# A 512-column bfloat16 product ahead of each PSUM bank of the RWKV features, scores and inverses

## The chip, the cores and the metric

The kernel runs on one core of one Trainium2 chip, in one launch. The metric is the device time of that core in microseconds (us), the median of the runs shown; lower is better. The engines are called as in the profile: PE (TensorE, its matmuls), PEld (its weight loads), DVE (VectorE), ACT (ScalarE), POOL (GpSimd) and SP (SyncE, which issues transfers).

## The reference, cut to what matters

Two layers of a block that mixes 512 latent tokens and 256 context tokens of width 1024 by three mixers side by side (RWKV, S5 and window attention), and then sends them through 32 experts of which each token takes two. The part that the change touches is the RWKV mixer: 4 heads of width 64, in both directions of time.

```python
def step(s, inp):
    r_t, w_t, k_t, v_t, kk_t, b_t = inp
    s_kk = jnp.einsum('bhvk,bhk->bhv', s, kk_t)
    s = s * w_t[:, :, None, :] - s_kk[..., None] * b_t[:, :, None, :] + v_t[..., None] * k_t[:, :, None, :]
    return s, (jnp.einsum('bhvk,bhk->bhv', s, r_t) if emit else None)
```

The kernel doesn't scan token by token: it works in chunks of 64 tokens, for which it needs decayed features, triangular score matrices and the inverse of one of them.

## The kernel before, in words

A layer runs in this order: the input side (projections `proj` and S5), then one stage that holds RWKV, attention, the modulation products of later stages (`mod_unit`, which streams `w_mod` in slices of 128 columns) and the output mix, then the experts. In that stage everything lies in one program whose order on each engine a planner makes from the dependences; the calls only give the order in which the work is written down.

RWKV itself (`rwkv`, from line 327) goes over six tiles of 128 tokens, written down as tiles 0, 1, 2, 5, 3, 4:

- `front(i)`, line 367: the features of a tile. It takes six PSUM banks in turn: the two low-rank products against `wa` (lines 382 and 388, 512 columns each), two banks of transposes (line 59), the running sum of the decay (line 416) and its chunk totals (line 422, 2 columns). ACT, DVE and POOL work between them.
- `back(i)`, line 465: the scores of a tile. Five banks for each direction: two of transposes (line 59, copied out by ACT at lines 483 and 495), two of scores (line 503, masked by DVE at line 506) and one for the score times the values (line 515).
- `inverse(b)`, line 524: the inverses of the 32x32 triangles of three tiles in each direction, on DVE and POOL (lines 551 and 552).
- `solve(i, d)`, line 564: four banks, in which the inverses are put together to 64x64 (lines 585 and 592) and applied (lines 604 and 606).
- `step(n, d)`, `output` and `finish`, from line 616: the recurrence over 12 chunks in each direction, and what is written from it.

Every bank comes from `bank()`, line 46. It gives a tile of 128x512 float32 of the stream that is set: `FS` (`b_f`, 2 buffers) for `front`, `finish` and direction 0 of `solve` and `step`, `GS` (`b_g`, 2 buffers) for `back` and direction 1, `b_a` (4 buffers) for attention, modulation and the mix. A bank can be written again when the readers of its tile before have released it. `oneb` is a 128x128 bfloat16 tile of ones in SBUF.

`fill` (line 2167) writes down attention, modulation and mix work between the tiles of RWKV, so PE has other work in the same stage.

Of the kernel before, what the change touches and what calls it, by code (L numbers as in the profile page):

```python
# [10 lines left out]
F32 = mybir.dt.float32  # L11
# [19 lines left out]
class K:  # L31


    def __init__(self, tc, a):
        self.tc, self.nc, self.a = tc, tc.nc, a
        self.dr = {}
        self.win = {}
        self.free = []
        self.stream = ('m', 8)

    def dram(self, name, shape, dt=F32):
# [3 lines left out]

    def bank(self):

        return self.ps.tile([128, 512], F32, name='b_' + self.stream[0], tag='b_' + self.stream[0], bufs=self.stream[1])

    def pool(self, name, st, **kw):  # L50

# [3 lines left out]
def tr(k, out, x):  # L55

    n = x.shape[0]
    r = x.base_partition()
    k.nc.tensor.transpose(out, x, k.idf[r:r + n, r:r + n])  # L59
# [265 lines left out]
def rwkv(k, l, st, cvd, Y, ys, streams, fill):  # L325
# [40 lines left out]

    def front(i):

        out = emit_ctx or i >= 2
        k.stream = FS  # L370
        Cv = Fp.tile([128, 8, 128], F32, name='cvt', bufs=3)
# [85 lines left out]
        for d in range(2):  # L457
# [3 lines left out]
                q.dma_start(rec[z, :, r:r + 64, c:c + 256], src)  # L461
            nc.sync.dma_start(atd[z, :, 0], at[:, d, :])
        F[i] = at, rh, bt, kh

    def back(i):

        out = emit_ctx or i >= 2
        k.stream = GS
        at, rh, bt, kh = F.pop(i)
        n = 2 if out else 1  # L470
        j = len(done) % 2
        done.append(i)
        vv = vz[j]
        nc.scalar.dma_start(vv[0:64], rec[slot[i, 0], :, 0:64, 256:512].rearrange("c t x -> t c x"))
        for d in range(2):
            z = slot[i, d]

            ar = Fp.tile([128, 2, 2, 2, 64], F32, name='ar', bufs=2)
            p = k.bank()
            for s, src in ((0, at), (1, rh))[0:n]:  # L480
                for q in range(2):
                    tr(k, p[:, 256 * s + q * 128:256 * s + q * 128 + 128], src[:, d, q * 128:q * 128 + 128])
                A.copy(ar[:, s].rearrange("p c q t -> p q c t"), p[:, 256 * s:256 * s + 256].rearrange("p (q c t) -> p q c t", q=2, c=2))
            if out:
                nc.scalar.dma_start(rec[z, :, :, 640:768].rearrange("c p x -> p c x"), ar[:, 1].rearrange("p c q t -> p c (q t)"))

            bk = bz[(2 * j + d) % 2]
            p = k.bank()
            for s, src in ((0, bt), (1, kh)):
                for q in range(2):  # L490
                    tr(k, p[:, 256 * s + q * 128:256 * s + q * 128 + 128], src[:, d, q * 128:q * 128 + 128])
                pv = p[:, 256 * s:256 * s + 256].rearrange("p (q c t) -> p q c t", q=2, c=2)
                for hp in range(2):
                    r_ = slice(64 * hp, 64 * hp + 64)
                    A.copy(bk[r_, hp, :, :, 1 - s, :], pv[r_])  # L495

            sc = Fp.tile([128, 2, 2, 2, 2, 64], F32, name='sc', bufs=2)
            for hp in range(2):
                p = k.bank()
                pv = p.rearrange("p (c q s t) -> p c q s t", c=2, q=2, s=2)  # L500
                for q in range(2):
                    for cp in range(2):
                        nc.tensor.matmul(pv[:, cp, q, 0:n, :], bk[:, hp, q, cp].rearrange("p s t -> p (s t)"),  # L503
                                         ar[:, 0:n, cp, q, :], start=True, stop=True)
                for s in range(n):
                    V.tensor_tensor(sc[:, s, :, hp], pv[:, :, :, s, :], k.msk[d][:, None, s:s + 1, :].to_broadcast([128, 2, 2, 64]), op=ALU.mult)
            nc.sync.dma_start(sca[z].rearrange("a p t -> p a t"), sc[:, 0].rearrange("p c h q t -> p (c h q) t"))
            if out:
                nc.sync.dma_start(rec[z, :, :, 768:1024].rearrange("c p x -> p c x"), sc[:, 1].rearrange("p c h q t -> p c (h q t)"))

            p = k.bank()
            for h in range(4):
                q, hp = divmod(h, 2)
                for cp in range(2):
                    nc.tensor.matmul(p[64 * cp:64 * cp + 64, 64 * h:64 * h + 64], sc[:, 0, cp, hp, q, :], vv[:, cp, 64 * h:64 * h + 64], start=True, stop=True)
            r1 = Fp.tile([128, 256], F32, name='r1', bufs=2)
            A.copy(r1, p[:, 0:256])
            nc.scalar.dma_start(atd[z, :, 1], r1)

    def dblk(ap, s0, q):  # L520

        return bass.AP(tensor=ap.tensor, offset=ap.offset + s0 * 4096 + 2080 * q, ap=[[4096, 24], [64, 32], [1, 32]])
# [40 lines left out]

    def solve(i, d):

        k.stream = (FS, GS)[d]
        z = slot[i, d]
        s0 = z * 8
        u, v = 64 + 32 * d, 32 - 32 * d
        ab = Q.tile([128, 8, 32], F32, name='ab', bufs=SB)  # L570
        nc.sync.dma_start(ab[u:u + 32], sca[z, :, u:u + 32, v:v + 32].rearrange("a p t -> p a t"))
        at = Q.tile([128, 2, 256], F32, name='atl', bufs=SB)
        nc.scalar.dma_start(at, atd[z])
        x = Q.tile([128, 4, 64], F32, name='x', bufs=SB)
        for cp in range(2):
            nc.sync.dma_start(x[64 * cp:64 * cp + 64], inv_o[s0 + 4 * cp:s0 + 4 * cp + 4].rearrange("h i t -> i h t"))
        t = Q.tile([128, 8, 32], F32, name='xt', bufs=SB)
        nc.scalar.dma_start(t[u:u + 32], inv_t[s0:s0 + 8].rearrange("h i t -> i h t"))

        p = k.bank()  # L580
        w = Q.tile([128, 4, 32], F32, name='xw', bufs=2)
        for cp in range(2):
            v = 64 * cp + 32 - 32 * d
            for h in range(4):
                nc.tensor.matmul(p[v:v + 32, 32 * h:32 * h + 32], ab[u:u + 32, 4 * cp + h, :],
                                 t[u:u + 32, 4 * cp + h, :], start=True, stop=True, tile_position=(u, v))
            A.copy(w[v:v + 32], p[v:v + 32, 0:128].rearrange("p (h t) -> p h t", h=4))
        p = k.bank()
        for cp in range(2):
            u, v = 64 * cp + 32 * d, 64 * cp + 32 - 32 * d  # L590
            for h in range(4):
                nc.tensor.matmul(p[u:u + 32, 32 * h:32 * h + 32], w[v:v + 32, h, :], x[v:v + 32, h, 32 - 32 * d:64 - 32 * d],
                                 start=True, stop=True, tile_position=(v, u))
            V.tensor_scalar(x[u:u + 32, :, 32 - 32 * d:64 - 32 * d], p[u:u + 32, 0:128].rearrange("p (h t) -> p h t", h=4), -1.0, None, op0=ALU.mult)
        own = [slice(0, 64), slice(64, 128)]
        heads = [(hq, 2 * (hq % 2) + hq // 2) for hq in range(4)]

        xa = Q.tile([128, 2, 128], F32, name='xa', bufs=2)
        W = Q.tile([128, 2, 256], F32, name='W', bufs=1)
        for cp in range(2):  # L600
            p = k.bank()
            for hq, h in heads:
                hp, q = divmod(hq, 2)
                nc.tensor.matmul(p[64 * hp:64 * hp + 64, 64 * q:64 * q + 64], at[own[cp], 0, 64 * h:64 * h + 64], x[own[cp], hq, :], start=True, stop=True)
            for hq, h in heads:
                nc.tensor.matmul(p[64:128, 256 + 64 * h:320 + 64 * h], x[own[cp], hq, :], at[own[cp], 1, 64 * h:64 * h + 64], start=True, stop=True)
            A.activation(xa[:, cp], p[:, 0:128], AF.Copy, scale=-1.0)
            V.tensor_scalar(W[64:128, cp], p[64:128, 256:512], -1.0, None, op0=ALU.mult)
        nc.scalar.dma_start(rec[z, :, :, 512:640].rearrange("c p x -> p c x"), xa)
        nc.sync.dma_start(rec[z, :, 64:128, 256:512].rearrange("c t x -> t c x"), W[64:128])  # L610

    chain = (tuple(range(12)), (3, 2, 1, 0, 11, 10, 9, 8, 7, 6, 5, 4))
    S = [None, None]
# [128 lines left out]
    def solves(b, j):  # L742
        for d in range(2):
            solve(batches[b][d][j], d)

    ahead = (0, 1, 2, 5, 3, 4)
    front(0)
    for j, i in enumerate(ahead):
        if j < 5:
            front(ahead[j + 1])  # L750
            fill('front')
        if i == 4:
            inverse(0)
        back(i)
        fill('back')
# [1329 lines left out]
def trunk(tc, a, out):  # L2085
    k = K(tc, a)
    nc = k.nc
    with ExitStack() as st:
# [50 lines left out]
        for l in range(2):  # L2139
# [12 lines left out]
            with ExitStack() as s1:  # L2152
# [26 lines left out]

                k.rest = k.normed = False  # L2180
                rwkv(k, l, s1, dr['cvd'], Y, ys, (('f', 2), ('g', 2)), fill)
                k.stream = ('a', 4)
                while not k.rest:
# [86 lines left out]
```

## Time and profile before

| what | value |
|---|---|
| median of 3 runs | 2898.29 us |
| range of the runs | 2891.7 to 2900.19 us |
| the profiled execution: time | 2882.98 us |
| the profiled execution: span | 2881.2 us |
| mean granted clock of PE over the span | 0.871 |
| PE busy | 2219.2 us (77%) |
| DVE, POOL, ACT busy | 1185.8, 823.0, 523.3 us |

The span is the time from the first to the last instruction of the profiled execution; its time is 1.8 us longer. A granted clock of 1.00 is 2.4 GHz and one of 0.50 is 1.2 GHz; a value between them is a mean over a stretch. "Busy" counts instructions that run, and an engine that waits is idle. PE executes in its program's order: while one instruction waits, all behind it wait.

### The profile page before, as it was taken

What the parts mean: (1) busy time and instruction counts of PE and PEld (TensorE: products, weight loads), DVE (VectorE), ACT (ScalarE), POOL (GpSimd) and SP (SyncE); (2) the same over time, 40 slices, a digit from 0 to 9 for tenths busy, and PEclk for the clock granted to TensorE, in tenths of its full rate; (3) what the DMA queues carried; (4) which work ended last, traced back from release to release, by engine and by line L of the source; (5) the groups of instructions that cost most, each with busy time, mean ns of one, the idle gap of its engine ahead of it and who ended that gap; (6) DMA issues with size and microseconds to landing.
All of it is one profiled execution on the core that took longest, in us unless ns stands there. A gap on an engine that the chain in (4) does not pass through costs nothing. (4 is left out here: it accounts for less than half of the span.)

```text
span 2881.2 us, 43454 instructions
## 1 busy us (share of the span) xinstructions
PE 2219.2 (77%) x16189; PEld 1487.5 (52%) x16189; DVE 1185.8 (41%) x2830; ACT 523.3 (18%) x1264; POOL 823.0 (29%) x1131
## 2 busy tenths in 40 slices
PE   5898677789874978989955787677898488788882
PEld 4786445567432544555525675455555254454441
DVE  7872554665556100000016873456645711111113
ACT  3222233223001100001015222233110100000001
POOL 2651322431544011101016652333324510111002
PEclk8999788789986999999987898579699699999996
DMA  8334466665627899989974324446784589998995
GB/s 241 93 94 116 141 179 185 175 189 163 220 93 265 351 418 371 391 329 379 388 279 121 83 56 142 117 128 161 212 244 140 230 355 418 416 379 331 384 419 201
DMA packets 404797, 691.34 MB, mean 240 GB/s; under 512 B 134755, under 2 KB 310627, under 8 KB 388097
## 3 DMA queue, kind: packets, MB, share of 16 engines
q1 hardware_dynamic: 311808, 600.10, 58.1%
q10 hardware_dynamic: 78880, 64.32, 7.5%
q0 software_dynamic: 13792, 22.61, 2.1%
q8 instruction: 211, 3.46, 0.5%
q14 instruction: 106, 0.86, 0.1%
HBM read 607.98 MB, written 95.44 MB: 244 GB/s over the span
## 5 line engine op out<-in xcount | busy, mean ns | idle before, releaser
L1762 PE MATMUL b_m<-w,xT 128*64 128x256 f32 x4928 | 593.7, 396 | 128.8 <-DMA w<-in_expert_w_gate_dram 80.2
L1762 PEld LDWEIGHTS b_m<-w,xT 128*64 128x64 f32 x4928 | 391.9, 142 | 333.3 <-issue 148.0
L243 PE MATMUL b_m<-xT,win 128*128 128x256 f32 (+1 forms) x1416 | 275.8, 355 | 7.0 <-POOL xT L167 3.5
L243 PEld LDWEIGHTS b_m<-xT,win 128*128 128x128 f32 x1416 | 232.8, 202 | 41.0 <-POOL xT L167 4.4
L1786 PE MATMUL b_m<-w,aT 128*64 128x512 f32 x1024 | 231.0, 592 | 1.1 <-issue 0.6
L1775 DVE COPY aT<-b_m 128x256 f32<-128x256 f32 x64 | 27.2, 425 | 474.4 <-PE b_m L59 474.4
L1792 POOL DMA_INDIRECT yb<-y,dx x64 | 63.9, 998 | 419.7 <-DVEq L1907 245.2
L1786 PEld LDWEIGHTS b_m<-w,aT 128*64 128x64 f32 x1024 | 76.2, 137 | 117.3 <-issue 108.3
L1764 ACT ACTIVATE act<-b_m 128x256 f32<-128x256 f32 x64 | 24.6, 384 | 566.8 <-PE b_m L1762 566.8
L1765 DVE TENSOR_TENSOR act<-act,b_m 128x256 f32<-128x256 f32 x64 | 27.0, 422 | 233.5 <-PE b_m L1762 233.5
L877 PE MATMUL b_a<-kz,qb 128*128 128x128 f32 (+2 forms) x416 | 111.9, 415 | 8.2 <-ACT pr L898 6.1
L1582 PE MATMUL b_a<-wo,yt 128*128 128x512 f32 x240 | 112.4, 618 | 0.0
L1792 POOL DMA_INDIRECT yb<-yo,dx x13 | 12.9, 994 | 291.7 <-ACTq L1907 166.2
L127 PE MATMUL b_a<-wmod,cc 128*32 128x128 f32 x1280 | 64.2, 315 | 40.0 <-DMA wmod<-in_w_mod_dram 28.0
L877 PEld LDWEIGHTS b_a<-kz,qb 128*128 128x128 f32 x416 | 78.2, 237 | 32.2 <-issue 13.0
L59 PE MATMUL b_a<-idf,pr 128*128 128x128 f32 x320 | 58.4, 304 | 34.3 <-DVE pt L921 11.5
L503 PE MATMUL b_g<-ar,bz 128*128 128x128 f32 (+1 forms) x384 | 66.2, 337 | 11.7 <-ACT bz L495 11.6
L1855 POOL DMA_INDIRECT xg<-hd,ix x32 | 33.0, 1031 | 146.8 <-PE b_m L59 105.2
L503 PEld LDWEIGHTS b_g<-ar,bz 128*128 128x128 f32 x384 | 61.8, 248 | 22.3 <-ACT bz L495 18.0
L1582 PEld LDWEIGHTS b_a<-wo,yt 128*128 128x128 f32 x240 | 45.2, 196 | 51.2 <-issue 50.3
L127 PEld LDWEIGHTS b_a<-wmod,cc 128*32 128x32 f32 x1280 | 37.7, 122 | 58.0 <-DMA wmod<-in_w_mod_dram 29.9
L551 POOL TENSOR_TENSOR tl<-Bm,Xh 112x4 f32<-112x4 f32 (+13 forms) x112 | 38.0, 339 | 95.0 <-DVE Xh L552 53.7
(539 smaller groups left out, 3979.9 us busy)
## 6 DMA issues: line engine op xcount, KB each, us to landing
w<-in_expert_w_gate_dram SPq DMA_DIRECT2D x64, 2048.0 KB
w<-in_expert_w_up_dram SPq DMA_DIRECT2D x64, 2048.0 KB
w<-in_expert_w_down_dram SPq DMA_DIRECT2D x64, 2048.0 KB
wmod<-in_w_mod_dram SPq DMA_DIRECT2D x80, 512.0 KB
rec<-rec SPq DMA_DIRECT2D x40, 512.0 KB
win<-in_w_in_dram SPq DMA_DIRECT2D x16, 1024.0 KB
wmod<-in_w_mod_dram SPq DMA_DIRECT2D x4, 2048.0 KB
sca<-sc SPq DMA_DIRECT2D x24, 256.0 KB
```

The source lines that it names most:

```text
L59: k.nc.tensor.transpose(out, x, k.idf[r:r + n, r:r + n])
L127: nc.tensor.matmul(p[32 * g:32 * g + 32, :], k.cc[:, kk, :], wt[:, kk, :], start=kk < 4, stop=kk >= 4, tile_position=(0, 32 * g))
L243: nc.tensor.matmul(p[:, :n], wt[u][:, kk, j * 128:j * 128 + 128], xT[v][:, kk, c0:c0 + n], start=kk == 0 and q == 0, stop=kk == 7 and q == 2)
L503: nc.tensor.matmul(pv[:, cp, q, 0:n, :], bk[:, hp, q, cp].rearrange("p s t -> p (s t)"), ar[:, 0:n, cp, q, :], start=True, stop=True)
L551: eng.tensor_tensor(t[:, 0:n, j:32], Bm[:, r0:r1, j:j + 1].to_broadcast([112, n, w]), x.to_broadcast([112, n, w]), op=ALU.mult)
L877: nc.tensor.matmul(dst, qb[:, 2 * v + e, :], kz[:, v, r, 128 * keys[c][0]:128 * keys[f - 1][0] + 128], start=c == 0 or (c == 4 and r == 0) ...
L1582: nc.tensor.matmul(ps[h], y[:, kt, :], wo[:, kt, 512 * h:512 * h + 512], start=kt == 0, stop=kt == 5)
L1762: mm = nc.tensor.matmul(p[64 * h:64 * h + 64, 0:256], xT[:, kk, :], w[:, kk, 256 * h:256 * h + 256], start=kk == 0, stop=kk == 7)
L1775: k.nc.vector.tensor_copy(aT, pa[:, 0:256].rearrange("p (j x) -> p j x", j=2))
L1786: nc.tensor.matmul(py[64 * s:64 * s + 64, :], aT[:, j, 64 * h:64 * h + 64], wd[:, q, 512 * s:512 * s + 512], start=q == 0, stop=q == 3)
L1792: sc = nc.gpsimd.indirect_dma_start(out=yb, out_offset=bass.IndirectOffsetOnAxis(ap=dst, axis=0), in_=y, in_offset=None, bounds_check=3071 ...
L1855: return nc.gpsimd.indirect_dma_start(out=out, out_offset=None, in_=hd, in_offset=bass.IndirectOffsetOnAxis(ap=idx, axis=0), bounds_check= ...
```

## The change

A field `dense` says how many extra products `bank()` issues into the bank that it hands out. It is 1 inside `front`, `back` and `solve` and 0 elsewhere. The extra product multiplies the ones tile by itself, four times side by side, so that it writes all 512 columns of the bank in one bfloat16 matmul; it begins a group of its own (`start=True`), and the products of the bank that follow begin theirs anew, so what it wrote is overwritten or never read. No other line changes.

```diff
+        self.dense = 0
 ...
     def bank(self):
 
-        return self.ps.tile([128, 512], F32, name='b_' + self.stream[0], tag='b_' + self.stream[0], bufs=self.stream[1])
+        b = self.ps.tile([128, 512], F32, name='b_' + self.stream[0], tag='b_' + self.stream[0], bufs=self.stream[1])
+        for _ in range(self.dense):
+
+            self.nc.tensor.matmul(b, self.oneb, self.oneb[:, None, :].to_broadcast([128, 4, 128]), start=True, stop=True)
+        return b
 ...
     def front(i):
 
+        k.dense = 1
 ...
         F[i] = at, rh, bt, kh
+        k.dense = 0
 
     def back(i):
 
+        k.dense = 1
 ...
             nc.scalar.dma_start(atd[z, :, 1], r1)
+        k.dense = 0
 ...
     def solve(i, d):
 
+        k.dense = 1
 ...
         nc.sync.dma_start(rec[z, :, 64:128, 256:512].rearrange("c t x -> t c x"), W[64:128])
+        k.dense = 0
```

## Rows read from the trace of the kernel before

**Rows 1.** The page: busy time of PE, and its granted clock in 40 slices.
```profile
PE 2219.2 (77%) x16189; PEld 1487.5 (52%) x16189; DVE 1185.8 (41%) x2830; ACT 523.3 (18%) x1264; POOL 823.0 (29%) x1131
PEclk8999788789986999999987898579699699999996
```

**Rows 2.** Windows by stage: length, PE busy (count), granted clock, DMA share, GB/s.
```profile
277.00:484.00 207.00, 137.21 (x1057) 0.78 0.59 165
484.00:533.00 49.00, 34.65 (x310) 0.86 0.70 189
533.00:720.00 187.00, 162.13 (x1833) 0.85 0.64 177
1766.00:1994.00 228.00, 167.29 (x1136) 0.74 0.47 131
2012.00:2100.00 88.00, 72.19 (x896) 0.75 0.72 206
2100.00:2232.00 132.00, 113.85 (x973) 0.92 0.66 192
```

**Rows 3.** What PE waited for from 277 to 506: total us, times, longest.
```profile
PE b_f L416 <- ACT rk L397: 7.0, 1, 7.0
PE b_g L503 <- ACT bz L495: 6.3, 4, 3.4
PE b_g L59 <- ACT bz L495: 6.1, 4, 3.4
PE b_f L388 <- ACT e L442: 3.7, 1, 3.7
PE b_f L416 <- DVE sg L345: 3.2, 1, 3.2
PE b_f L382 <- ACT gc L424: 2.2, 2, 1.9
PE b_g L515 <- DVE sm L904: 1.8, 1, 1.8
```

**Rows 4.** PE's timeline around one such wait: start, length, operation, count, idle before.
```profile
301.59 2.08 PE L416 MATMUL b_f<-sg,cum 128*128 128x256 f32 x4 [7.03 <-ACT rk L397]
303.46 1.71 PE L422 MATMUL b_f<-blk,sg 128*128 128x2 f32 x8
```

**Rows 5.** Windows: the granted clock around that wait and in a busy stretch of layer 1.
```profile
298.00:300.00 2.00, 0.00 (x0) 0.58 0.12 49
302.00:304.00 2.00, 2.00 (x8) 0.50 0.14 48
308.00:310.00 2.00, 2.00 (x16) 0.86 0.33 106
1788.00:1798.00 10.00, 9.20 (x34) 0.50 0.40 113
1816.00:1830.00 14.00, 12.81 (x53) 0.50 0.38 97
1830.00:1854.00 24.00, 20.19 (x82) 0.50 0.40 109
```

**Rows 6.** PE's timeline in that busy stretch.
```profile
1816.38 3.68 PE L503 MATMUL b_g<-ar,bz 128*128 128x64 f32 x16 [0.46 <-ACT bz L495]
1823.24 1.87 PE L422 MATMUL b_f<-blk,sg 128*128 128x2 f32 x8
1824.97 0.67 PE L59 MATMUL b_g<-idf,e 128*128 128x128 f32 x2
1829.01 2.08 PE L388 MATMUL b_f<-wa,cvt 128*128 128x512 f32 x2 [0.81 <-DVE sg L384]
```

**Rows 7.** PE's timeline: line 388 once more, and products like the added one.
```profile
274.60 1.02 PE L388 MATMUL b_f<-wa,cvt 128*128 128x512 f32 x2
1737.81 4.01 PE L243 MATMUL b_m<-xT,win 128*128 128x512 f32 x17
1858.76 0.28 PE L883 MATMUL b_a<-br,idb 128*128 128x128 bf16 x2
```

**Rows 8.** Windows: the granted clock of the products of line 243.
```profile
1737.80:1742.00 4.20, 4.02 (x18) 1.00 0.00 0
```

**Rows 9.** One line's instructions: min, median, max ns; first and last start.
```profile
L382 PE MATMUL b_f<-wa,cvt x24: 592/1061/1167, 273.6 to 1891.8; 128*128 128x512 f32 x24
L883 PE MATMUL b_a<-br,idb x48: 219/219/314, 466.5 to 2059.9; 128*128 128x128 bf16 x48
L585 PE MATMUL b_f<-xt,ab x192: 191/191/258, 533.2 to 2170.6; 32*32 32x32 f32 x192
```

**Rows 10.** What ACT's queue did ahead of the copy of line 397.
```profile
294.79 5.61 ACTq L461 DMA_DIRECT2D rec<-av  x1
300.97 0.57 ACT L397 COPY rk<-b_f 128x512 f32<-128x512 f32 x1
```

## The prediction

> **What bounds the kernel now.** I read the page first, then windows by stage, then what PE waits for, then its timeline. The page shows PE busy for 77% of the span, far ahead of every other engine, and its clock granted at 0.5 to 0.9 in the slices of the two RWKV stages [rows 1]. The chain that ended last reaches back only through the last 18 us, so it says nothing of these stages; the windows have to. In them [rows 2] two kinds of stretch differ. While fronts and backs run (277 to 484 in layer 0, 1766 to 1994 in layer 1) PE is busy for 137 of 207 us and 167 of 228 us: no engine is full, and what sets the pace is the round trip from PE to ACT or DVE and back. While solves and steps run (533 to 720, 2012 to 2232) PE is busy for 82 to 87% of the time, and it is close to being the bound. The experts come after and only shift.
>
> The waits of the first kind [rows 3] are of two sorts, and the difference matters for a product that needs no input. In one, PE waits because a bank has not been released: line 416 for the copy out of the bank of line 59 two banks earlier (7.0 us), line 59 for bz (6.1), line 388 for the exponentials (3.7), line 382 for gc (2.2), together 19.0 us. In the other it waits for the input of a product: line 503 for bz (6.3), line 416 for sg (3.2), line 515 behind DVE (1.8), together 11.3 us.
>
> The timeline and fine windows show what such a wait does to the clock. PE idles from about 294.6 to 301.59 [rows 4]; the clock falls to 0.50 inside the wait and returns only in the slice 308 to 310, so everything between runs at 1.2 GHz [rows 5]. Layer 1 is worse: from 1788 to 1854 the clock stays at 0.50, though PE is busy for 12.8 of 14 us in one part of it [rows 5]. What runs there is short products: 64 columns at line 503, 2 columns at line 422, transposes at line 59, with only now and then a product of 512 columns [rows 6]. So being busy with these has not raised it.
>
> **The price of one added product.** The trace of before holds no 512-column bfloat16 product. The nearest rows are the 512-column products of line 243, 17 in 4.01 us, 0.236 us each in a stream [rows 7] at a granted clock of 1.00 [rows 8], and the 128-column bfloat16 product of line 883: two in 0.28 us of which one lasts 0.219 [rows 9], so 0.06 us more for 128 columns and 0.24 for 512. Both give 0.24 us at the upper level. At the lower, the same pair of products at line 388 takes 2.08 instead of 1.02 us [rows 6, 7], and line 422 1.7 to 1.9 us, so I take 0.45 us. The weight load of the ones lies beside the product before, and the bank's own load beside the added one; I count neither.
>
> **How many.** A front takes 6 banks, a back 10, a solve 4. Per layer that is 36 + 60 + 48 = 144, over both layers 192 in fronts and backs and 96 in solves, 288 in all. Line 382's 24 matmul rows, two for each front, bear out the 12 fronts [rows 9]. Nothing is removed, no transfer is added, and the order of banks within a stream stays. The wait for a bank's release moves from its first product to the added one.
>
> **The sum with the clock as it is.** A granted clock of 0.78 means 44% of the time at the lower level, 0.74 means 52% (twice the distance from 1), 0.85 30%, 0.75 50%, 0.92 16% [rows 2]. With 0.24 and 0.45 us mixed accordingly, 96 products in layer 0's fronts and backs are 32 us and 96 in layer 1's 33.5; 48 in layer 0's solves are 14.5 and 48 in layer 1's 14.9. That is 95 us of PE.
>
> Not all of it lies on the path. In fronts and backs the product is free where the bank is there but the input isn't (the 11.3 us sort) and where PE is idle for other streams; it costs its full time where the bank was late (the 19.0 us sort), because it then stands between the release and the first product. I put 0.45 of it on the path. In the solve stretch PE has little idle time and a queue of attention and modulation work that the product delays; a solve also waits for ACT between its banks, and a product can lie there. I put 0.65 on the path. So 0.45 x 65.5 + 0.65 x 29.4 = 48.6 us. The bounds are 0 (all of it in idle time) and 95 (none of it).
>
> **What the clock can give back.** Time at the lower level is 0.44 x 207 = 91, 0.52 x 228 = 119, 0.30 x 187 = 56, 0.50 x 88 = 44 and 0.16 x 132 = 21 us. PE is busy in them for about the stretch's share (0.66, 0.73, 0.87, 0.82, 0.86): 60, 87, 49, 36 and 18 us. The same work at the upper level takes 1/1.8 of it (line 388 shows 2.0; line 585's short products, 191 to 258 ns, far less [rows 9]), so 0.44 of it goes: 27 + 38 us in fronts and backs, 21 + 16 + 8 in the solve stretches. With the same path shares 29 + 29 = 58 us, if no time at the lower level were left, and the added products would then cost 0.24 each, 35.7 us on the path instead of 48.6.
>
> With f the share of that time that disappears, the change in time is 48.6 - 12.9 f - 58 f = 48.6 - 71 f. It breaks even at f = 0.68.
>
> **Which f.** In favour: from 1816 to 1830 about nine banks are opened, so some 4 us of long products would stand among the short ones, and the climb back should come sooner. Against: the clock falls in waits, and the longest of them are for a bank. In the wait of 7.03 us the added product waits with everything else: ACT is stuck for 5.61 us in the issue of a transfer and copies the bank at 300.97 [rows 10]. It cannot keep the clock up there. So I expect earlier climbs and nearly as many falls: f about one half, which gives 48.6 - 35.5 = +13 us.
>
> The Trainium skill ("TensorE: Matmul & The Clock Gate", section "A second HAM failure mode: psum-queue depth-cycling") speaks against the change: in a kernel of 512-column bfloat16 products that cycles through PSUM banks, PE idles a little between groups and the clock keeps going down and up. By that rule f would be near 0. No row of before shows such a product in these streams.
>
> **The sum.** The profiled execution took 2882.98 us, 1.8 us more than its span, and lies 15.3 us below the median of the runs; with +13 it would be 2896, and the median 2898.3 + 13 = 2911 us.
>
> **Rivals.** *The clock comes back* (faster). The added products end most of the time at the lower level; the long stretch from 1788 to 1854 goes. With f = 0.9 the change is -15 us, 2883 us; with f = 1, -22. It decides from f = 0.68, and measurably from 0.81. For it: PE runs in that stretch, only with short products. Against: the waits for banks stay. The Trainium skill, same page, section "Why this matters for your kernels", asks for no long idle gaps between bursts of matmuls; the trace agrees that the clock falls in such a gap.
>
> *No gain of clock* (slower). f = 0.1 gives +41 us, 2940 us. For it: the clock stayed down through PE time that was almost full. Against: what filled it was short.
>
> *PE's queue is held* (slower). The planner can put an added product, which needs no input, ahead of attention or modulation work, and the bank comes later than it planned; then all of that waits. Forty such holds of 0.9 us, each shorter than the waits of 2 to 7 us that exist, on top of a break-even would be about +36 us, 2934 us. It needs the planner to be wrong often.
>
> *Nothing measurable*: f between 0.56 and 0.81, within 8.7 us of before. I take 0.3% as about what a measurement of this kernel can tell from no change.
>
> **How the numbers follow.** Chances: forecast (f from 0.3 to 0.56, +9 to +27 us) 0.30; no gain of clock 0.10; queue held 0.08; nothing measurable 0.24; clock comes back 0.28. So slower 0.48, same 0.24, faster 0.28. The forecast's own range is 2907 to 2925. The range that should hold the time 8 times in 10 reaches down to f = 1 and a little beyond for a path share that is too small, 2874, and up to f = 0, +48, 2946.
>
> **What would show it.** 288 rows at the line in `bank()` of about 0.24 and 0.45 us between starts. The granted clock in the front and back stretches up from 0.78 and 0.74 to about 0.88, with the fall near the ACT copy of rk still there. The first `solve` product later or earlier than 533 says what fronts and backs lost or won. The forecast is wrong if the clock in layer 1's long stretch is at 1.00 and that stage is shorter, or if the clock has not moved at all.

## The result, and the profile after

The changed kernel takes 2925.65 us (median of 4 runs, 2920.17 to 2929.86) against 2894.99 us of before (4 runs, 2886.06 to 2900.19): a ratio of 1.0101, 95% interval 1.0077 to 1.0126. It is slower, by 30.7 us where the forecast had 13; 2925.65 lies in the range given and above the forecast's own one. The profiled execution took 2920.17 us, 1.8 more than its span, and 5.5 below its median; that of before lay 12 below the median of these runs, so the two profiles are 37.2 us apart.

The page, the same two rows as [rows 1]:

```profile
PE 2268.6 (78%) x16477; PEld 1502.8 (51%) x16477; DVE 1191.9 (41%) x2830; ACT 526.2 (18%) x1264; POOL 830.1 (28%) x1131
PEclk8999898789886999999987898797699789999996
```

288 matmuls more, yet PE is busy for only 49.4 us more: the rest of its work runs faster. The windows by stage, shifted to the new starts, answer to [rows 2]; the last is the long stretch of [rows 5], 24 us later as the whole layer is:

```profile
277.00:484.00 207.00, 145.89 (x1109) 94.00 (x1107) 104.06 (x231) 64.64 (x195) 63.51 (x91) 0.84 0.58 165
484.00:530.00 46.00, 37.74 (x340) 25.06 (x338) 33.32 (x98) 14.64 (x45) 25.58 (x74) 0.89 0.56 140
530.00:720.00 190.00, 162.90 (x1685) 120.36 (x1684) 105.20 (x296) 52.50 (x178) 46.73 (x121) 0.84 0.63 177
1790.00:2012.00 222.00, 168.54 (x1184) 120.69 (x1183) 129.86 (x287) 78.56 (x225) 80.21 (x139) 0.83 0.47 130
2030.00:2118.00 88.00, 77.29 (x776) 52.55 (x778) 44.75 (x135) 16.85 (x60) 27.19 (x76) 0.67 0.65 180
2118.00:2270.00 152.00, 129.35 (x1150) 80.81 (x1151) 72.02 (x155) 19.77 (x64) 53.33 (x48) 0.93 0.65 193
...
1812.00:1878.00 66.00, 45.19 (x242) 32.27 (x242) 36.05 (x63) 20.54 (x54) 28.66 (x32) 0.72 0.39 110
```

That stretch in before:

```profile
1788.00:1854.00 66.00, 48.90 (x196) 34.90 (x196) 32.78 (x59) 20.10 (x53) 25.33 (x31) 0.50 0.42 117
```

After the length come busy time and count of PE, PEld, DVE, ACT and POOL, then the granted clock, the DMA share and GB/s. In fronts and backs the clock rose from 0.78 to 0.84 and from 0.74 to 0.83, and the long stretch of layer 1 has 0.72 instead of 0.50. In the solves it did not rise; in layer 1's first 88 us it fell, from 0.75 to 0.67.

The added products by their line (min, median, max ns; first and last start):

```profile
L52 PE MATMUL b_g<-oneb x168: 376/389/634, 272.0 to 2217.1; 128*128 128x512 bf16 x168
L52 PE MATMUL b_f<-oneb x120: 376/389/634, 271.5 to 2212.1; 128*128 128x512 bf16 x120
```

All 288 are there. One lasts 376 to 389 ns at the upper level and 634 at the lower, but the next product starts before its end. PE's timeline at the wait of [rows 4] (line 422 here is 416 of before):

```profile
297.47 0.38 PE L52 MATMUL b_f<-oneb 128*128 128x512 bf16 x1 [2.04 <-ACT rk L403]
297.69 1.02 PE L422 MATMUL b_f<-sg,cum 128*128 128x256 f32 x4
```

Line 422 starts 0.22 us after the added product. The wait for the copy of rk has moved to the added product, as foreseen, but it lasts 2.04 us instead of 7.03, and line 422 takes 1.02 us instead of 2.08, so at the upper level.

To compare kernels I cut each layer at three starts: the first product of a front, the first of a solve (line 585 of before, 595 here), the first of the experts. Front to solve is stretch A, solve to experts is stretch B:

| us | A, layer 0 | B, layer 0 | A, layer 1 | B, layer 1 |
|---|---|---|---|---|
| before | 259.6 | 396.6 | 247.3 | 299.7 |
| after | 257.2 | 423.1 | 241.0 | 321.1 |
| difference | -2.4 | +26.5 | -6.3 | +21.4 |

The four sum to +39.2, the rest of the program makes -2.0 of the 37.2. So fronts and backs, where I expected most of the loss, gained, and the solve stretches lost all of it.

Where layer 0's 26.5 us begin is seen in PE's timeline. The changed kernel:

```profile
719.51 3.70 PE L1593 MATMUL b_a<-wo,yt 128*128 128x512 f32 x8
723.19 17.41 PE L1593 MATMUL b_a<-wo,yt 128*128 128x512 f32 x40
...
744.52 0.63 PE L616 MATMUL b_g<-atl,x 64*64 64x64 f32 x8
...
793.77 1.97 PE L64 MATMUL b_a<-idf,h 128*128 128x128 f32 x8 [15.15 <-DVE h L1658]
...
832.12 32.99 PE L1593 MATMUL b_a<-wo,yt 128*128 128x512 f32 x72
```

Line 1593 is the output mix, an attention-side work of the same stage. Its first block (24 products, 48 rows) holds PE from 719.5 to 740.6, and solves go on behind it: the last product of line 616 starts at 760.3. In before the last solve product started at 720.9 and the same block at 722.1, behind it. Nothing waits for an added product there. The planner, given 288 instructions more, has put the rest of the program in another order.

### The profile page after: what moved, and what is told of

The parts are those of the page before. It is cut to its first block, busy times and chain, and to the rows that moved or that the text cites. A ratio compares the mean times of both kernels' runs of the same rounds, so it can differ in the third digit from the quotient of the medians.

```text
span 2918.4 us, 43908 instructions
## 1 busy us (share of the span) xinstructions
PE 2268.6 (78%) x16477; PEld 1502.8 (51%) x16477; DVE 1191.9 (41%) x2830; ACT 526.2 (18%) x1264; POOL 830.1 (28%) x1131
## 5 line engine op out<-in xcount | busy, mean ns | idle before, releaser
L248 PE MATMUL b_m<-xT,win 128*128 128x256 f32 (+1 forms) x1416 | 273.5, 353 | 8.4 <-POOL xT L172 3.7
L888 PE MATMUL b_a<-kz,qb 128*128 128x128 f32 (+2 forms) x416 | 101.0, 385 | 5.9 <-ACT pr L909 2.5
L1803 POOL DMA_INDIRECT yb<-yo,dx x13 | 12.9, 993 | 289.1 <-ACTq L1918 165.3
L52 PE MATMUL b_g<-oneb 128*128 128x512 bf16 x168 | 72.5, 435 | 24.1 <-ACT r L525 8.8
L888 PEld LDWEIGHTS b_a<-kz,qb 128*128 128x128 f32 x416 | 72.3, 220 | 24.3 <-issue 7.5
L52 PE MATMUL b_f<-oneb 128*128 128x512 bf16 x120 | 53.0, 447 | 20.0 <-ACT rk L403 12.9
```

Source lines behind the costliest of these rows:

```text
L52: self.nc.tensor.matmul(b, self.oneb, self.oneb[:, None, :].to_broadcast([128, 4, 128]), start=True, stop=True)
L248: nc.tensor.matmul(p[:, :n], wt[u][:, kk, j * 128:j * 128 + 128], xT[v][:, kk, c0:c0 + n], start=kk == 0 and q == 0, stop=kk == 7 and q == 2)
L888: nc.tensor.matmul(dst, qb[:, 2 * v + e, :], kz[:, v, r, 128 * keys[c][0]:128 * keys[f - 1][0] + 128], start=c == 0 or (c == 4 and r == 0) ...
L1803: sc = nc.gpsimd.indirect_dma_start(out=yb, out_offset=bass.IndirectOffsetOnAxis(ap=dst, axis=0), in_=y, in_offset=None, bounds_check=3071 ...
```

## The experiments

Every run is compared with runs of the kernel before on the same chip. Three theories:

- **Price**: the added products' PE time on the path (the prediction's main term).
- **Held**: an added product waits for its bank, and PE waits with it.
- **Order**: the planner's new order of the other work costs, whatever the products last.

All runs, with the stretches as above; "block" says where layer 0's first mix block starts in the trace: behind the last solve product, ahead of it, or between (most of its products behind the solves, or interleaved with them).

| run | added products | block | A0 | B0 | A1 | B1 | median us | ratio, 95% |
|---|---|---|---|---|---|---|---|---|
| e1_front_back | fronts, backs | behind | 259.2 | 396.7 | 241.5 | 302.2 | 2893.77 | 0.9962, 0.9938 to 0.9987 |
| e2_solve | solves | ahead | 260.5 | 422.6 | 247.9 | 314.4 | 2932.9 | 1.0117, 1.0091 to 1.0143 |
| e3_short | all, 8 columns | ahead | 273.5 | 430.7 | 251.4 | 306.3 | 2937.87 | 1.0124, 1.0096 to 1.0151 |
| e4_double | all, two a bank | ahead | 269.9 | 426.1 | 246.5 | 317.1 | 2939.97 | 1.0157, 1.0116 to 1.0198 |
| f5_late | all | between | 259.3 | 416.9 | 244.2 | 324.2 | 2923.94 | 1.0096, 1.0068 to 1.0124 |
| f6_early | none | ahead | 263.7 | 426.8 | 248.3 | 304.6 | 2923.21 | 1.0088, 1.0056 to 1.0119 |
| f7_l1_solves | all but layer 0's solves | behind | 259.6 | 396.6 | 242.1 | 322.2 | 2911.2 | 1.0047, 1.0025 to 1.0069 |
| f8_fb_short | fronts, backs, 8 columns | ahead | 265.4 | 414.8 | 247.2 | 305.1 | 2927.44 | 1.011, 1.0084 to 1.0137 |
| g1_order | all | between | 254.3 | 412.6 | 242.4 | 321.8 | 2910.82 | 1.0039, 1.002 to 1.0057 |
| g2_l1_fb | layer 1's fronts, backs | behind | 262.3 | 401.7 | 241.4 | 307.5 | 2892.35 | 0.997, 0.9953 to 0.9987 |
| h1_order_only | none | between | 262.9 | 410.1 | 247.4 | 301.6 | 2906.66 | 1.004, 1.002 to 1.0061 |
| h2_l0_solves | all but layer 1's solves | between | 256.6 | 410.3 | 241.2 | 301.9 | 2895.66 | 1.0002, 0.9986 to 1.0017 |

Each stretch is from one profile. The expert products of layer 0 alone took 544 to 562 us from their first start to their last, with no pattern that follows the products, and the profile lies up to 15 us from its median. Where PE runs the same rows in the same order, or all but the same, a stretch still scatters: A0 from 259.6 to 263.7 us (before, e2, f6, g2, h1), B1 from 299.7 to 305.1 (before, f6, f8, h1); and e3_short and f8_fb_short, alike in A in products and order, lie 8.1 us apart in A0 and 4.2 in A1. So a total is taken from the medians, and a stretch is trusted where several kernels agree.

### Parts of the change

**e1_front_back**: fronts and backs keep the product, solves lose it.

```diff
     def solve(i, d):
 
-        k.dense = 1
+        k.dense = 0
```

> The long product stands in front of the banks of fronts and backs alone, 192 of 288. If the price of the products on PE sets the time, with f about one half in these stretches, it is 29 us of price less some 5 for the clock's cheaper products and 15 for the clock: +5 to +10 us against before. If the loss of the change is the solves' (the first solve of the changed kernel starts 4 us earlier than before in layer 0 and 6 us earlier in layer 1, counted from the layer's first front), it is -4 to -10 us. If it is the planner's new order of the whole stage, it is anywhere within 30 us of before, without a relation to the count.

**e2_solve**: the other part alone (in `front` and `back` the line becomes `k.dense = 0`).

> The long product stands in front of the 96 banks of solves alone. By the price on PE: 96 x 0.24 to 0.45 us, 0.65 of it on the path, +15 to +25 us. If the loss is the solves' alone, about +30, the whole of it. If it is the planner's order, no relation to the count.

**e3_short**: all 288 products, of 8 columns.

```diff
-            self.nc.tensor.matmul(b, self.oneb, self.oneb[:, None, :].to_broadcast([128, 4, 128]), start=True, stop=True)
+            self.nc.tensor.matmul(b[:, 0:8], self.oneb, self.oneb[:, 0:8], start=True, stop=True)
```

> All 288 extra products, but 8 columns instead of 512, so the waits for banks and the place in the queue stay and PE's time nearly goes. By the price on PE and the clock: between 0 and +8 us, and the granted clock of the front and back stretches back at about 0.78 and 0.74. If the loss comes from a product that waits for its bank in PE's queue, it stays at about +30. If it comes from the planner's order, it can be anything, since the planner counts the short products as cheap and orders anew.

**e4_double**: two a bank (`k.dense = 2` in all three places).

> Two long products in front of each bank instead of one, 576. By the price on PE with some more clock: about twice the loss less the clock's gain, +50 to +70 us, and the granted clock of the front and back stretches near 0.90. If the loss is one of waiting, which a second product behind the first doesn't add to: about +30 to +40.

Measured: fronts and backs alone make the kernel 0.4% faster than before. Solves alone make it 1.2% slower, with the whole of the loss in B0 (+26.0 against before) and B1 (+14.7). With 8 columns B0 loses more (+34.1) than with 512, and with twice the products no more than with one (+29.5 against +26.5): in layer 0 the loss does not follow the PE time of the products. In layer 1 it does begin with it: 8 columns leave B1 at 306.3, 512 columns bring it to 321.1. Layer 0 speaks for order, layer 1 for price. The totals of e3_short and e4_double, 37 and 39 us above before, would fit held as well. But held is small in the solves: in the profile after, the idle time ahead of the added product while layer 0's solves run is 0.4 us for ACT and 0.2 for DVE in all.

### The order, with and without products

In layer 0 the calls write the mix down between steps; a table, `FILL`, says how many items of (attention, modulation, mix) follow each step. The next runs change its last entries, for layer 0 alone.

**f6_early**: the kernel before, without any added product, its last entries changed.

```diff
-(0, 2, 2), (0, 2, 0), (0, 0, 5)
+(0, 2, 0), (0, 2, 2), (0, 0, 5)
```

The planner then has the block ahead of the last solves. (The two items are written one step later by this edit, not earlier as the expectation says; what counts is where the planner puts them.)

> The kernel before, with no added product at all, but with the two mix items written one step earlier in layer 0, so that PE has the block of 24 mix products ahead of the last 16 of the 96 last-line solve products. Order theory: the same loss without any added product: the stretch from the first solve product to the first expert product of layer 0 goes from 397 to 412 to 425 us, the time 15 to 27 us above before. Price theory: 395 to 399 us and within 5 us of before.

Measured: B0 is 426.8 us, +30.2, without one added product; the time is 0.88% above before. The timeline has the pattern of the changed kernel (line 1582 is 1593 there, 1635 and 59 are 1646 and 64):

```profile
743.03 17.43 PE L1582 MATMUL b_a<-wo,yt 128*128 128x512 f32 x40
...
760.68 0.45 PE L606 MATMUL b_f<-atl,x 64*64 64x64 f32 x5
...
804.86 1.97 PE L59 MATMUL b_a<-idf,h 128*128 128x128 f32 x8 [16.13 <-DVE h L1647]
...
842.04 32.84 PE L1582 MATMUL b_a<-wo,yt 128*128 128x512 f32 x72
```

So an order with the block ahead costs, without any product, as much as layer 0 lost (30.2 and 26.5 us; the two orders are alike, not the same in every row). **f7_l1_solves** has 240 of the 288 products, none of them in layer 0's solves (`k.dense = l` in `solve`, l being the layer), and the block stays behind.

> Products in all fronts and backs and in layer 1's 48 solve banks, none in layer 0's. PE's order in layer 0 keeps the mix behind the last solves. Order theory for layer 0: its stretch is 395 to 400 us as before. Price in layer 1, where PE has little idle time: its stretch from the first solve product to the first expert product is 314 to 322 us against 300 in before, so the whole is 2 to 10 us above before, against 7 us below with products in fronts and backs alone. If layer 1's loss is no price but needs layer 0's products, its stretch is about 302 us and the time 5 to 10 us below before.

Measured: B0 is 396.6 us, that of before, and B1 322.2, all of the loss; the time is 13.5 us above before, 3.5 more than expected. The timeline of its layer 0, for the same work:

```profile
726.23 18.27 PE L1593 MATMUL b_a<-wo,yt 128*128 128x512 f32 x42
...
749.40 1.98 PE L1646 MATMUL b_a<-wo,yo 128*128 128x512 f32 x4
...
758.24 1.16 PE L64 MATMUL b_a<-idf,h 128*128 128x128 f32 x8 [2.19 <-DVE h L1658]
...
803.01 33.20 PE L1593 MATMUL b_a<-wo,yt 128*128 128x512 f32 x72
```

The two timelines differ above all by a wait: PE's transposes of `h`, the first normalised tile of the mix, wait 15.15 us (changed kernel) or 16.13 (f6_early), here 2.19. `h` is DVE's. DVE in the changed kernel, the last of whose input products (line 1646) started on PE at 751.22:

```profile
783.10 1.27 DVE L1652 TENSOR_TENSOR q<-b_a,q 128x512 f32<-128x512 f32 x2
...
792.44 1.28 DVE L1658 SCALAR_TENSOR_TENSOR h<-h,r_sb,hb 128x1024 f32<-128x1024 f32 x1
```

and in f7_l1_solves:

```profile
749.95 0.68 DVE L1652 TENSOR_TENSOR q<-b_a,q 128x512 f32<-128x512 f32 x1
...
756.90 1.28 DVE L1658 SCALAR_TENSOR_TENSOR h<-h,r_sb,hb 128x1024 f32<-128x1024 f32 x1
```

In the changed kernel DVE takes that norm up 32 us after the last of these products started. Ahead of it in DVE's order stands what the late solves feed, the recurrence and its outputs; DVE is busy for 18.5 of these 32 us and mostly waits for PE's products of the recurrence in the rest. PE has 4.8 us of work in the slice from 780 to 800. The second mix block, 72 rows in 33 us, starts 29.1 us later (832.1 instead of 803.0), and the first expert product 22.1 us later (952.7 instead of 930.6), so some of the delay is made up behind the block. The other 4.4 of the 26.5 us of B0 are only that its solves began earlier (529.6 instead of 534.0). That is the way: block ahead of the last solves, recurrence late on DVE, norm behind it, second block late, experts late.

**f5_late** keeps all 288 products and writes the two mix items two steps later:

```diff
-(0, 2, 2), (0, 2, 0), (0, 0, 5)
+(0, 2, 0), (0, 2, 0), (0, 0, 2), (0, 0, 5)
```

> The changed kernel with all its 288 products, but in layer 0 the program writes the first two items of the mix (24 products) after the last two solves instead of ahead of them. Order theory: the loss in layer 0 comes from the block of mix products that stands on PE ahead of the last solves; so the stretch from the first solve product to the first expert product of layer 0 goes from 423 us (changed kernel) back to 397 to 408 us, and the time to 8 to 18 us above before. Price theory: the loss is the PE time of the added products, which are all still there; the stretch stays at 420 to 425 us and the time about 30 us above before.

**g1_order** does the same with seven items in that step:

```diff
-(0, 2, 2), (0, 2, 0), (0, 0, 5)
+(0, 2, 0), (0, 2, 0), (0, 0, 7), (0, 0, 5)
```

> The changed kernel with all its products; layer 0's first two mix items are written two steps later, and that step takes seven items, so that from there on as many items are written as before. Order theory: the last solve product of layer 0 comes as early as in the run with late mix items (about 742 us), the recurrence ends at about 865 us, and now the mix follows without the 25 us lost there: layer 0's stretch from the first solve product to the first expert product is 397 to 408 us, the time 10 to 20 us above before, of which layer 1's solves make 18. Price theory: 415 to 423 us in layer 0 and about 27 us above before.

Measured: in f5_late the last solve product comes at 742.2 instead of 760.3, but B0 is 416.9, far from the 397 to 408 that order expected, and the time, 26.3 us above before, is nearer to what price expected. The table gives fewer mix items up to that step, so the end of the mix came late instead (its last row starts at 884.7, that of g1_order at 847.5): one loss was put in the place of another, and the run says little. g1_order makes up for the items: B0 412.6, last solve product 742.7, second block at 813.9, and the time is 0.39% above before, where the changed kernel has 1.01%. The time is in the range that order expected, B0 is 5 us above it. What remained could be the price in layer 0 or the place of the block, which is still not that of before. **h1_order_only** has its writing without any product (the same line in the kernel before), **h2_l0_solves** its writing with all products but those of layer 1's solves (`k.dense = 1 - l` in `solve`).

> The kernel before without any added product, with the mix items of layer 0 written as in the run that restored their place. If that rewriting gains nothing by itself, layer 0's stretch from the first solve product to the first expert product is 395 to 402 us and the time within 5 us of before; then the 413 us with all products are the price of layer 0's 48 solve products. If the rewriting itself costs, the stretch is 405 to 413 us and the time 8 to 16 us above before, and these products cost next to nothing.

> Products in all fronts and backs and in layer 0's 48 solve banks, none in layer 1's; mix items of layer 0 written as in the run that restored their place. Price in layer 0 with the mix kept behind most of the last solves: its stretch from the first solve product to the first expert product is 408 to 415 us against 397, layer 1's about 302, and the time 3 to 9 us above before (10 to 16 above products in fronts and backs alone). If PE time in layer 0's solves costs nothing once the order is mended: 397 to 402 us and 4 to 10 us below before.

Measured: B0 is 410.1 us without a product, 410.3 and 412.6 with 48 in it. In B0, h2_l0_solves and g1_order have PE's order all but row for row; that of h1_order_only is near, with about 85 of 100 rows in the same order. So at a like order, not the same one, the 48 products of layer 0's solves cost 0 to 2.5 us, which is within the scatter of a stretch. In h2_l0_solves the granted clock over B0 is 0.83 against 0.80 in h1_order_only, and PE is busy for 312.7 us against 313.3: the other work ran as much faster as the products took. The new writing alone costs 13.5 us of B0 and 0.4% of the time.

### The clock in fronts and backs

**f8_fb_short**: fronts and backs alone, 8 columns (the edits of e1_front_back and e3_short together). **g2_l1_fb**: 512 columns in layer 1's fronts and backs alone (`k.dense = l` in `front` and `back`, 0 in `solve`).

> Products of 8 columns in fronts and backs alone (192), none in solves. The planner here puts the mix block ahead of the last 20 solve products of layer 0, as in the four slower kernels. Order theory: layer 0's stretch from the first solve product to the first expert product is 418 to 430 us though no solve has an added product; layer 1's about 302. Clock: without long products the stretch from the first front product to the first solve product is 8 to 14 us longer in layer 0 and 3 to 8 in layer 1 than with 512 columns (259 and 241 us); the time 30 to 42 us above before. Price theory: short products cost at most 0.07 us each, layer 0's stretch stays at 397 us, and the time is 0 to 10 us above before.

> Products of 512 columns in layer 1's fronts and backs alone (96 of the 288); PE's order of solves and mix in layer 0 stays that of before. If these products pay through the clock, layer 1's stretch from the first front product to the first solve product is 240 to 243 us against 247 in before at a granted clock of about 0.83 against 0.74, everything else stays, and the time is 4 to 9 us below before. If the gain of products in fronts and backs came from another planned order, the stretch is 246 to 249 us and the time is that of before.

Windows of A in both layers (length, PE busy, granted clock); first e1_front_back, 512 columns:

```profile
272.20:531.40 259.20, 183.79 (x1445) 0.84 0.58 159
1778.60:2020.10 241.50, 176.74 (x1258) 0.82 0.49 132
```

f8_fb_short, the same products with 8 columns:

```profile
272.40:537.80 265.40, 176.41 (x1462) 0.79 0.58 163
1806.80:2054.00 247.20, 178.27 (x1277) 0.76 0.49 137
```

e2_solve, none:

```profile
273.10:533.60 260.50, 183.10 (x1374) 0.76 0.60 168
1794.20:2042.10 247.90, 174.51 (x1188) 0.76 0.49 136
```

The long products are 6 us better than the short ones in each layer (in layer 0 less than the 8 to 14 expected), at a clock of 0.84 and 0.82 against 0.79 and 0.76, though they are more work. Over the six kernels with 512 columns A0 is 254.3 to 259.6 (mean 257.7), over the five without 259.6 to 263.7 (261.8); A1 is 241.0 to 244.2 in seven (242.0) against 247.3 to 248.3 in four (247.7; before, e2, f6, h1). So fronts and backs gain 4.1 and 5.7 us. f8_fb_short also has the block ahead, no product in a solve, and a B0 of 414.8, +18.2, somewhat less than order expected. g2_l1_fb gives A1 241.4 and 0.3% less time with PE's order in layer 0 all but that of before, so the gain doesn't need the moved block.

Inside A1, however, PE's order changed with the long products. Compared by line and tiles, the other work has one and the same order, row for row, in all seven kernels with 512 columns there; of the 1184 rows of before 928 keep their order in it, and 18 attention rows (line 934 of before) have moved behind the first solve, some 2.8 us of PE by an estimate from 8 rows of that line in 1.24 us in f7_l1_solves. With 8 columns 1152 rows keep theirs. So no run parts the clock from the order inside fronts and backs. A1 of g2_l1_fb, and of h1_order_only, which has no product:

```profile
1776.90:2018.30 241.40, 174.56 (x1258) 0.83 0.49 132
```

```profile
1784.70:2032.10 247.40, 174.60 (x1185) 0.75 0.50 137
```

PE is busy for as long with the products as without: its other work took less time by what they took, at a clock of 0.83 instead of 0.75. The 6 us gained are idle time (66.8 instead of 72.8 us), and whether the clock or the order saved it is not shown.

Two products a bank (e4_double) bring the clock in A to 0.87 and 0.88, but A is 269.9 and 246.5, in yet another order of PE: past one product the kernel loses again, and PE is busy for 198.5 and 189.4 us of A instead of the 183.8 and 176.7 of e1_front_back.

### Layer 1's solves

B1 is 314.4 to 324.2 us (mean 320.7) in the five kernels with one 512-column product in these solves and 299.7 to 307.5 (mean 303.2) in the seven without: 17.5 us for 48 products, 0.36 each, about all of their PE time. All of B1 in f7_l1_solves, and in h2_l0_solves, which has no product there:

```profile
2021.40:2343.70 322.30, 243.40 (x2086) 0.78 0.63 197
```

```profile
2018.70:2320.50 301.80, 217.46 (x2040) 0.81 0.67 210
```

PE is busy for 25.9 us more and idle for 5.4 us less; from start to next start the products take 0.38 us each (an estimate from the 44 that lie in the stretch), some 17 us, and the rest is other work at a lower clock. The first 88 us of it, the changed kernel, f7_l1_solves, h2_l0_solves (none), e3_short (8 columns) and e4_double, a fence each:

```profile
2030.40:2118.00 87.60, 77.29 (x776) 0.67 0.65 181
```

```profile
2021.40:2109.00 87.60, 79.61 (x784) 0.64 0.65 183
```

```profile
2018.70:2106.00 87.30, 70.96 (x862) 0.75 0.74 209
```

```profile
2065.30:2153.00 87.70, 71.08 (x867) 0.75 0.70 202
```

```profile
2049.30:2137.00 87.70, 73.18 (x861) 0.90 0.75 210
```

With the products PE is busy for 77 to 80 of 88 us instead of 71, gets through some 85 matmuls less, and its clock is granted at 0.67 and 0.64 instead of 0.75. With 8 columns nothing changes; with two products the clock is at 0.90, and B1 is 4 us shorter than with one. So the sums say that the price of one product is paid here, and that the clock adds to it. But PE's order differs here too: in the changed kernel the first modulation product comes 31.8 us after the first solve product, in before 0.9 us, and of the 2022 rows of B1 in before 1534 keep their order. No run has that order without the products, so price is what the sums speak for, and order is not ruled out.

## Why the prediction was right, and where it was wrong

The sign was right, by two errors that cancel in part, and so the time fell into the range by luck and not by the sum. Split by its own terms, with f one half, the prediction had fronts and backs at 0.45 x 65.5 minus half of 29 + 8.8 (the 12.9 us split as the products are), so +10.6, and the solves at 0.65 x 29.4 minus half of 29 + 4.1, so +2.5. The profile has -8.7 and +47.9.

- **Bounds and count**: right. 288 products; 0.22 us from one start to the next at the upper level, where 0.24 was taken. At the lower, two of e4_double in a row last 1.06 us, of which one is 0.634, so 0.43 where 0.45 was taken. One small slip: layer 1's solves, weighted by the lengths of the two stretches, come to 14.5 us and not 14.9.
- **Path share 0.45 in fronts and backs**: far too high for the clock's return that goes with it. The clock's share at the lower level fell from 0.44 to 0.32 and from 0.52 to 0.34, so f was about 0.3, less than the half assumed; by the formula that would be +18 us, and the stretch gained 10 over all runs. Over A1 PE was busy for as long as without the products (174.5 us in the mean of either group) and idle for 6 us less: the other work gave back all that they took, more than the formula has for this f. Over A0 it was busy for 6 us more and idle for 10 us less. So which of the two was off, the share or the return, can't be told, and PE's order changed with them.
- **The fall near the copy of rk "still there"**: wrong in this profile. The wait is 2.04 us and the clock stays up on both sides of it. It falls a little later, to 0.50 in the slice 308 to 310, behind a wait of 3.61 us for `bz`; why the copy came sooner was not tried.
- **Path share 0.65 in the solves, 19 us**: its size was about right in sum (0 to 2.5 in layer 0 and 17.5 in layer 1, if order has no part in it), its spread over the layers wrong, and f there was not one half: over B the clock is 0.82 in both kernels in layer 0 (0.80 to 0.83 at a like order, which paid for the products), and in layer 1 it fell from 0.80 to 0.79.
- **"Nothing is removed ... the order of banks within a stream stays"**: this is the step that failed, with a cost put at nothing for a new order. It is true within a stream, and I priced the change as if all other work kept its place. The order between streams changed, in layer 0 at the price of 26.5 us, more than the 17.7 by which the forecast missed. The rival *PE's queue is held* named the planner, but had an added product standing ahead of attention work and waiting for its bank. What happened is the reverse, mix work ahead of solves, and it needs no wait of an added product.
- **No gain of clock**: it rose in fronts and backs. The Trainium skill ("TensorE: Matmul & The Clock Gate", section "A second HAM failure mode: psum-queue depth-cycling") has a median of 379 ns for such a product at the upper level; the trace agrees (376 to 389). That the clock keeps going down and up between groups, as that section has it, shows in the profile after too (from 0.50 to 1.00 in slices of 6 us between 1788 and 1884), but is no reason here against the product: 0.84 and 0.83 with it, 0.78 and 0.74 without.

What stays open: how much of the gain in A and of the loss in B1 is PE's new order there; why the planner moves the block (8-column products do it too, and 192 of 512 columns do not); why the clock falls in layer 1's first solves with one product and rises with two; why e3_short has A0 at 273.5 and f8_fb_short, with the same products there and all but the same order, at 265.4; and the 13 to 16 us of B0 by which g1_order and h1_order_only are still above before. No run had the changed kernel in exactly the order of before, nor the kernel before in that of the changed one.

Two versions beat both kernels: products in fronts and backs alone (0.9962) and in layer 1's fronts and backs alone (0.997). Their intervals overlap.

## What to carry to other kernels

Where a planner orders the program, an added instruction isn't added to the old schedule but gives a new one; compare the order of the work around it in both traces before pricing the instruction, and make the control that has the new order without the instruction. Look at the order inside each stage too: here it changed in all four stretches, and where no such control was made the cause stays argued. Products that need no input were followed by a gain where PE idles in many short waits at the lower clock (4 to 6 us a stage), and in layer 1's solves, where PE has little idle time, by a loss of about their PE time. Price an addition by stage: this one gained in two stretches and lost in two.

## What the runs showed of the hardware

The granted clock did not move one way with more PE work: in the same 88 us of layer 1's solves it was 0.75 with no added product and with one of 8 columns, 0.64 to 0.67 with one of 512 in each bank, and 0.90 with two. In fronts and backs 8-column products left it at 0.79 and 0.76, 512 columns brought 0.84 and 0.82, and two of them 0.87 and 0.88. PE's order of the other work differs between these kernels, so the products are not shown to be the only cause.
